# A Mamba-2 and pooling block on one core: the row's sums multiplied in front of the product for the state instead of behind it

## The chip, the core and the metric

The kernel runs on one core of a Trainium2 chip. The metric is the device time of one execution in microseconds (us). The time of a kernel is the median of several executions.

## What is computed

One layer of a decoder. Each of the 1024 prompt rows, and 8 samples of 8 rows, is normalised, projected by one large matrix, and sent through two branches: a causal pooling and a state-space recurrence (SSD). The branches are gated, added, projected once more and added to the input. The part that matters here is the recurrence. It goes over the prompt in chunks of 128 rows:

```python
def step(h, inp):
    xq, dq, Bq, Cq = inp
    acs = jnp.cumsum(dq * Ag, axis=1)
    seg = acs[:, :, None] - acs[:, None, :]
    decay = jnp.exp(jnp.where(mask, seg, -jnp.inf))
    cb = jnp.einsum('bign,bjgn->bijg', Cq, Bq)
    att = cb[..., None] * decay * dq[:, None]
    y = jnp.einsum('bijge,bjgep->bigep', att, xq)
    y = y + jnp.einsum('bign,bige,bgepn->bigep', Cq, jnp.exp(acs), h)
    last = acs[:, -1]
    w_in = jnp.exp(last[:, None] - acs) * dq
    h = h * jnp.exp(last)[..., None, None] + jnp.einsum('bjgn,bjge,bjgep->bgepn', Bq, w_in, xq)
    return h, y
```

`y` is the row's sums: one product within the chunk and one with the state `h` of the chunk before. The last line is the new state. The 32 heads are in 4 groups of 8 heads, each with its own B and C of 128 states.

## The kernel before

The kernel is one program of about 25,400 instructions in stages: the conditioned norm, the large projection, the samples' recurrence beside its end, then the **chunk rows** (about 765 to 1055 us of the span), and the last projections. The change lies in the chunk rows.

There are 32 chunks, 4 groups times 8 chunks, one after the other. `chunk(g, c)` (L1497) is a generator; each call of `next` puts one part of one chunk into the program:

- Part 0 loads the decays (L1234, by `decays`), B and C (L1502) and x (L1505), all on SP's queue.
- Part 1 takes the exponentials: `cE` on ScalarE (L1509), the mask on GpSimd (`far`, L1238), eight exponentials on ScalarE (`exps`, L1242). In the very first chunk these come later.
- Part 2 transposes x and B on TensorE (L1516, L1518), multiplies B with C (L1519), copies B to SBUF on ScalarE (`bt`, L1521) and C to PSUM (L1523), and lets VectorE make `xd` (L1527), `xw` (L1529), `dec` times B and C (L1534) and `cE` times C (L1536).
- Part 3 holds the change. The product for the state, `pu`, is one matmul of 512 columns into PSUM (L1541), recorded as two passes. The row's sums, `pi`, are made by `inner` (L1249): for each pair of heads two matmuls of 128 columns by 64 rows of `xd` (L1254) and, from the second chunk of a group on, two more with the state of the chunk before (L1257). VectorE then adds `pu` to the scaled old state (L1549; GpSimd scales it, L1547; in a group's first chunk ScalarE copies instead, L1545), and adds the skip term to `pi` in four instructions (L1553).
- Part 4 is `finish`: gating on VectorE (L1469), copies and squares on ScalarE (L1471, L1472), and sums on GpSimd (L1473 to L1480).

Between the parts stand **pieces** of other products (`products`, L1830; matmuls at L221): 12 matmuls each of 352 or 384 columns into one of three PSUM banks, emptied by VectorE or ScalarE (L1724, L1742, L1745). They fill TensorE while the other engines prepare the next chunk. In each step of the loop (L1849) TensorE gets the transposes of the next chunk, then about one piece, then `pu` and `inner` of this chunk, then one or two pieces.

What sets the order: TensorE's and SP's instructions are bound to the order in which the program is written (`in_line(order)`, L1910, with `ORDER`, L1837). The order on VectorE, ScalarE and GpSimd is made by the planner, which runs the program against computed times (`schedule_with_timeline_sim`, L19) and takes what is ready, earlier program text first.

Buffers: `pu` has one PSUM bank (`psC`), the transposes and `pi` share four (`psB`), the pieces have three (`psA`). `xw` has one SBUF buffer, so `xw` of the next chunk waits until this chunk's `pu` has been multiplied. `cE`, `xd` and the state have two, `dec` three.

Of the kernel before, what the change touches and what calls it, by code (L numbers as in the profile page):

```python
# [20 lines left out]
P = 128  # L21
# [25 lines left out]
def tile_pool_ssd_step(  # L47
# [8 lines left out]
    def nm(s):  # L56
        uid[0] += 1
        return f"{s}_{uid[0]}"
# [34 lines left out]
    def Y4(pool, dt=F32R):  # L93
        return pool.tile([P, 4, T], dt, tag="Y", name=nm("Y"), bufs=2)

    def PB():
        return psB.tile([P, 512], F32, tag="ps", name=nm("ps"))
# [4 lines left out]
    def PC():  # L102

        return psC.tile([P, 512], F32, tag="pc", name=nm("pc"))
# [1127 lines left out]
    def decays(dec, g, c):  # L1232

        load(dec, acs_d[c, 8 * g:8 * g + 8, :].partition_broadcast(P))  # L1234

    def far(dec, c):

        nc.gpsimd.affine_select(dec, dec, [[0, 8], [1, P]], ALU.is_ge, FAR, base=0, channel_multiplier=-1)  # L1238

    def exps(dec, g, c):  # L1240
        for h in range(8):
            act(dec[:, h], dec[:, h], AF.Exp, bias=acT[:, c, 8 * g + h:8 * g + h + 1], scale=-1.0)  # L1242
# [6 lines left out]
    def inner(xd, dec, S, state=None, cE=None):  # L1249
        pi = PB()  # L1250
        for q in range(4):
            o = [pi[64 * hh:64 * hh + 64, q * S:(q + 1) * S] for hh in range(2)]
            for hh in range(2):
                mm(o[hh], xd[:S, 2 * q + hh, :], dec[:S, 2 * q + hh], start=True, stop=state is None)  # L1254
            for hh in range(2 if state is not None else 0):
                h = 2 * q + hh
                mm(o[hh], state[:, h * 64:h * 64 + 64], cE[:, h], start=False, stop=True)  # L1257
        return pi[:, :4 * S].rearrange("p (q i) -> p q i", i=S)
# [201 lines left out]
    hst = [None] * NG  # L1460
# [3 lines left out]
    def ckt(shape, tag, bufs=2):  # L1464
        return (cl if tag in CKL else ca if tag in ("dec", "xb", "cE", "bc") else ck).tile(list(shape), F32, tag=tag, name=nm(tag), bufs=bufs)

    def finish(g, o, S, v, sz, y=None):

        V.tensor_tensor(v, v if y is None else y, sz, ALU.mult)  # L1469
        yhc = yh[g][:, :, o:o + S]  # L1470
        act(yhc, v, AF.Copy)  # L1471
        act(sz, v, AF.Square)  # L1472
        nc.gpsimd.tensor_tensor(yl[g][:, :, o:o + S], v, yhc.bitcast(F32), ALU.subtract)  # L1473
        nc.gpsimd.tensor_tensor(sz[:, 0:2], sz[:, 0:2], sz[:, 2:4], ALU.add)
        sa = sq_acc[:, o:o + S]
        if g == 0:
            nc.gpsimd.tensor_tensor(sa, sz[:, 0], sz[:, 1], ALU.add)
        else:
            nc.gpsimd.tensor_tensor(sz[:, 0], sz[:, 0], sz[:, 1], ALU.add)
            nc.gpsimd.tensor_tensor(sa, sa, sz[:, 0], ALU.add)  # L1480
# [16 lines left out]
    def chunk(g, c):  # L1497
        o = c * P
        dec = ckt([P, 8, P], "dec", 3)
        decays(dec, g, c)  # L1500
        bc = ckt([P, 2, P], "bc", 3)
        load(bc, xbc_d[g][c][:, 4:6])  # L1502
        Bf, Cf = bc[:, 0], bc[:, 1]
        xb = ckt([P, 4, P], "xb", 5)
        load(xb, xbc_d[g][c][:, 0:4])  # L1505
        yield
        if c > 0:
            cE = ckt([P, 8, P], "cE")
            act(cE, dec, AF.Exp, scale=-1.0)  # L1509
        if g > 0 or c > 0:  # L1510
            far(dec, c)
            exps(dec, g, c)
            yield
        px = PB()
        for q in range(4):
            nc.tensor.transpose(px[:, q * P:(q + 1) * P], xb[:, q], ident)  # L1516
        pbc = PB()
        nc.tensor.transpose(pbc[:, :P], Bf, ident)  # L1518
        mm(pbc[:, P:2 * P], Bf, Cf, start=True, stop=True)  # L1519
        bt = ckt([P, P], "bt", 2)  # L1520
        act(bt, pbc[:, :P], AF.Copy)  # L1521
        if c > 0:
            act(pbc[:, 2 * P:3 * P], Cf, AF.Copy)  # L1523
        pxv = px.rearrange("p (h d) -> p h d", d=64)
        heads = slice(8 * g, 8 * g + 8)
        xd = ckt([P, 8, 64], "xd", 2)
        V.tensor_tensor(xd, pxv, dtT[:, c, heads].unsqueeze(2).to_broadcast([P, 8, 64]), ALU.mult)  # L1527
        xw = ckt([P, 8, 64], "xw", 1)
        V.tensor_tensor(xw, pxv, wdT[:, c, heads].unsqueeze(2).to_broadcast([P, 8, 64]), ALU.mult)  # L1529
        if g == c == 0:  # L1530
            yield
            far(dec, c)
            exps(dec, g, c)
        V.tensor_tensor(dec, dec, pbc[:, P:2 * P].unsqueeze(1).to_broadcast([P, 8, P]), ALU.mult)  # L1534
        if c > 0:
            V.tensor_tensor(cE, cE, pbc[:, 2 * P:3 * P].unsqueeze(1).to_broadcast([P, 8, P]), ALU.mult)  # L1536
        yield
        if c == 0:
            yh[g], yl[g] = [Y4(hs if g % 2 else hp) for _ in range(2)]
        pu = PC()  # L1540
        mm(pu, bt, xw.rearrange("p h d -> p (h d)"), start=True, stop=True)  # L1541
        pi = inner(xd, dec, P, *((hst[g], cE) if c > 0 else ()))
        hn = ckt([P, 512], "hst", 2)
        if c == 0:
            act(hn, pu, AF.Copy)  # L1545
        else:
            nc.gpsimd.tensor_tensor(hn.rearrange("p (h d) -> p h d", d=64), hst[g].rearrange("p (h d) -> p h d", d=64),  # L1547
                                    Elb[:, c, heads].unsqueeze(2).to_broadcast([P, 8, 64]), ALU.mult)
            V.tensor_tensor(hn, hn, pu, ALU.add)  # L1549
        hst[g] = hn  # L1550

        for q in range(4):
            V.scalar_tensor_tensor(pi[:, q], xb[:, q], Dv[:, 4 * g + q:4 * g + q + 1], pi[:, q], ALU.mult, ALU.add)  # L1553
        yield
        finish(g, o, P, xb, szs.pop(0), pi)
        if c == NC - 1:
            store_(new_ssm_p[g], hn)
# [125 lines left out]
    def to_chunks():  # L1683
        nonlocal right, ca
        right.__exit__(None, None, None)
        right = tc.tile_pool(name="ca", bufs=3, side="right", reuse_waits="tile")
        ca = right.__enter__()
        right_all.append(right)
        seq.extend(chunk(g, c) for g in range(NG) for c in range(NC))
        next(seq[0])  # L1690
# [427 lines left out]
    for half in range(2):  # L2118
        c = slice(half * 512, half * 512 + 512)
# [168 lines left out]
```

## Time and profile before

| | |
|---|---|
| median of 3 runs | 1221.38 us (1220.97 to 1222.25) |
| the profiled execution | 1221.1 us |
| its span, first to last instruction | 1219.4 us |
| mean granted TensorE clock | 0.999 |
| DMA | 257.47 MB, mean 211 GB/s |

The profile is one execution of the program taken by the hardware profiler. PE is TensorE's matmuls, PEld its weight loads (they overlap PE), DVE is VectorE, ACT is ScalarE, POOL is GpSimd and SP is SyncE, which issues loads. A row of the timeline gives the start in us, the time in us, engine, line, operation, what it writes and reads, shapes, how many instructions are merged in it, and in brackets the idle time of its engine just before with what ended it. Rows of TensorE are merged where equal ones follow each other, and matmuls are pipelined: their ends overlap, so that the distance from start to start is what one costs.

### The profile page before, as it was taken

What the parts mean: (1) busy time and instruction counts of PE and PEld (TensorE: products, weight loads), DVE (VectorE), ACT (ScalarE), POOL (GpSimd) and SP (SyncE); (2) the same over time, 40 slices, a digit from 0 to 9 for tenths busy, and PEclk for the clock granted to TensorE, in tenths of its full rate; (3) what the DMA queues carried; (4) which work ended last, traced back from release to release, by engine and by line L of the source; (5) the groups of instructions that cost most, each with busy time, mean ns of one, the idle gap of its engine ahead of it and who ended that gap; (6) DMA issues with size and microseconds to landing.
All of it is one profiled execution on the core that took longest, in us unless ns stands there. A gap on an engine that the chain in (4) does not pass through costs nothing.

```text
span 1219.4 us, 25387 instructions
## 1 busy us (share of the span) xinstructions
PE 1204.5 (99%) x9298; PEld 1125.7 (92%) x9298; DVE 934.2 (77%) x1555; ACT 655.4 (54%) x1491; POOL 758.7 (62%) x677
## 2 busy tenths in 40 slices
PE   9999999999999999999999999999999999999997
PEld 8879999999999999999989889988988888999885
DVE  6993788877989578876676564686878889679976
ACT  6864366565656556454544344556676656312435
POOL 1137868876978778663676766155677758422661
PEclk9999999999999999999999999999999999999999
DMA  9736355564565546443555556897889888585794
GB/s 352 302 136 212 134 159 180 159 226 151 170 182 187 169 145 191 135 144 127 200 200 193 181 189 209 303 327 260 260 261 287 289 275 285 184 311 177 233 210 152
DMA packets 165748, 257.47 MB, mean 211 GB/s; under 512 B 32048, under 2 KB 79928, under 8 KB 165624
## 3 DMA queue, kind: packets, MB, share of 16 engines
q1 hardware_dynamic: 89256, 163.38, 40.9%
q10 hardware_dynamic: 74064, 88.27, 21.2%
q0 software_dynamic: 2304, 4.20, 2.0%
q8 instruction: 73, 1.20, 0.4%
q14 instruction: 51, 0.42, 0.1%
HBM read 170.69 MB, written 85.10 MB: 210 GB/s over the span
## 4 chain that ended last, share of the span: by engine, by line
PE 85%; DVE 5%; DMA 4%; ACT 3%; issue 2%; POOL 1%; SPq 0%; ACTq 0%; DVEq 0%; POOLq 0%
PE mm L410 23%; PE ps L410 23%; PE mm L221 15%; PE pc L410 5%; PE ps L1254 2%; PE pc L1541 2%; PE ps L2041 2%; PE ps L2040 2%; PE ps L1257 2%; PE ps L2039 2%; DMA dec<-acs_d 1%; DMA Y<-in_w_ada 1%; PE ps L1516 1%; PE ps L956 1%; DVE tf L642 1%
## 5 line engine op out<-in xcount | busy, mean ns | idle before, releaser
L148 POOL TENSOR_TENSOR wlo<-rawA,whi 128x512 fp32r<-128x512 f32 x120 | 173.3, 1450 | 80.2 <-ACT whi L145 78.9
L221 PE MATMUL mm<-Y,whi 128*128 128x352 f32 (+1 forms) x960 | 195.7, 334 | 0.8 <-DVE G L1974 0.6
L148 POOL TENSOR_TENSOR wlo<-raw,whi 128x512 fp32r<-128x512 f32 x90 | 149.8, 1673 | 61.3 <-ACT whi L145 54.0
L221 PEld LDWEIGHTS mm<-Y,whi 128*128 128x128 f32 x960 | 159.1, 188 | 7.6 <-issue 4.5
L1088 DVE SCALAR_TENSOR_TENSOR GA<-GA,cvT,GA 128x1112 f32<-128x1112 f32 x72 | 134.4, 1871 | 0.1
L410 PE MATMUL mm<-Y,whi 128*128 128x272 f32 x800 | 119.0, 291 | 0.0
L410 PE MATMUL ps<-Y,whi 128*128 128x272 f32 x800 | 117.4, 289 | 0.0
L145 ACT ACTIVATE whi<-rawA 128x512 fp32r<-128x512 f32 x120 | 75.2, 627 | 76.6 <-PE ps L410 32.4
L145 ACT ACTIVATE whi<-raw 128x512 fp32r<-128x512 f32 x90 | 56.0, 628 | 100.5 <-DVE raw L347 27.4
L410 PEld LDWEIGHTS mm<-Y,whi 128*128 128x128 f32 x800 | 106.8, 188 | 2.8 <-issue 2.4
L410 PEld LDWEIGHTS ps<-Y,whi 128*128 128x128 f32 x800 | 107.0, 188 | 0.8 <-issue 0.7
L221 PE MATMUL mm<-Y,wlo 128*128 128x352 f32 (+1 forms) x480 | 98.5, 327 | 0.0
L1242 ACT ACTIVATE dec<-dec,acT 128x128 f32<-128x128 f32 x256 | 78.7, 389 | 33.9 <-POOL dec L1238 33.9
L221 PEld LDWEIGHTS mm<-Y,wlo 128*128 128x128 f32 x480 | 81.7, 188 | 0.0
L285 POOL TENSOR_TENSOR pw<-pw,ph 128x512 fp32r<-128x512 f32 x40 | 67.1, 1678 | 13.2 <-ACT ph L283 12.7
L1473 POOL TENSOR_TENSOR Y<-xb,Y 128x512 fp32r<-128x512 f32 x32 | 41.2, 1289 | 53.8 <-ACT Y L1471 53.8
L410 PE MATMUL mm<-G,whi 128*128 128x272 f32 x480 | 71.4, 290 | 0.0
L410 PE MATMUL ps<-G,whi 128*128 128x272 f32 x480 | 70.5, 289 | 0.0
L410 PE MATMUL ps<-Y,wlo 128*128 128x272 f32 x400 | 66.6, 288 | 0.0
L410 PE MATMUL mm<-Y,wlo 128*128 128x272 f32 x400 | 66.6, 288 | 0.0
L410 PEld LDWEIGHTS mm<-G,whi 128*128 128x128 f32 x480 | 64.0, 188 | 1.3 <-issue 1.1
L410 PEld LDWEIGHTS ps<-G,whi 128*128 128x128 f32 x480 | 64.2, 188 | 0.4 <-issue 0.3
(579 smaller groups left out, 3155.3 us busy)
## 6 DMA issues: line engine op xcount, KB each, us to landing
rawA<-in_w_in SPq DMA_DIRECT2D x62, 512.0 KB
dec<-acs_d SPq DMA_DIRECT2D x32, 512.0 KB
xbc<-GA ACTq DMA_DIRECT2D x24, 512.0 KB
Y<-wo SPq DMA_DIRECT2D x10, 1024.0 KB
pw<-in_w_ssm_out ACTq DMA_DIRECT2D x32, 256.0 KB
ws<-ph ACTq DMA_DIRECT2D x32, 256.0 KB
ws<-pw ACTq DMA_DIRECT2D x32, 256.0 KB
h<-in_state_ssm SPq DMA_DIRECT2D x32, 256.0 KB
```

The lines of the kernel that those rows point to most:

```text
L145: ins = act(hi[:, :, :ncols], raw[:, :, :ncols], AF.Copy)
L148: (eng or nc.gpsimd).tensor_tensor(lo[:, :, :ncols], raw[:, :, :ncols], hi[:, :, :ncols].bitcast(F32), ALU.subtract)
L221: mm(ps[:, :n], w[k // 4][h][:, k % 4, :], r[k][:, o:o + n], start=(j == 0), stop=(j == len(terms) - 1))
L285: nc.gpsimd.tensor_tensor(raw.bitcast(F32R), raw, hi.bitcast(F32), ALU.subtract)
L410: mm(p, w[j // 8][:, k], A(k, s)[j // 4 == 1], start=(j == 0), stop=(j == 11))
L1088: V.scalar_tensor_tensor(d[:, :n], rp[:, k:k + n], cvT[:, 24 * k + mc:24 * k + mc + 1], d[:, :n], ALU.mult, ALU.add)
L1242: act(dec[:, h], dec[:, h], AF.Exp, bias=acT[:, c, 8 * g + h:8 * g + h + 1], scale=-1.0)
L1254: mm(o[hh], xd[:S, 2 * q + hh, :], dec[:S, 2 * q + hh], start=True, stop=state is None)
L1257: mm(o[hh], state[:, h * 64:h * 64 + 64], cE[:, h], start=False, stop=True)
L1473: nc.gpsimd.tensor_tensor(yl[g][:, :, o:o + S], v, yhc.bitcast(F32), ALU.subtract)
L1541: mm(pu, bt, xw.rearrange("p h d -> p (h d)"), start=True, stop=True)
L2039: mm(ps, hi, y[:, k, c0:c0 + cw], start=(first and k == 0), stop=False)
```

## The change

Two lines of part 3 change places. Before, TensorE multiplies `pu` and then the row's sums; afterwards the row's sums and then `pu`. Since TensorE's order is bound to the program's, its instructions change places with them. Nothing else is edited.

```diff
         pu = PC()
+        pi = inner(xd, dec, P, *((hst[g], cE) if c > 0 else ()))
         mm(pu, bt, xw.rearrange("p h d -> p (h d)"), start=True, stop=True)
-        pi = inner(xd, dec, P, *((hst[g], cE) if c > 0 else ()))
```

## The prediction

> **What bounds the kernel now.** I read the page first, then the stretch of the chunk rows, then the waits there, then single instructions in order of time.
>
> ```profile
> span 1219.4 us, 25387 instructions
> PE 1204.5 (99%) x9298; PEld 1125.7 (92%) x9298; DVE 934.2 (77%) x1555; ACT 655.4 (54%) x1491; POOL 758.7 (62%) x677
> 765.00:1055.00 290.00, 288.49 (x2296) 256.53 (x2295) 232.80 (x396) 179.75 (x467) 181.99 (x210) 1.00 0.84 279
> 1005.00:1035.00 30.00, 29.77 (x234) 26.09 (x232) 27.75 (x49) 20.41 (x54) 25.89 (x29) 1.00 0.86 285
> ```
>
> The last two rows are stretches: length, then busy time of PE, PEld, DVE, ACT and POOL, granted clock, DMA share. All 32 chunks lie in the first. PE is busy 288.49 of 290 us at clock 1.00, so it sets the pace, and at most 1.51 us of idle PE can be won here. DVE is busy 80% of the stretch and 27.75 of 30 us in its densest part: the engine that could become the bound.
>
> ```profile
> PE ps L1518 <- DVE cE L1536: 0.6, 1, 0.6
> PE mm L221 <- DVE Y L1572: 0.3, 1, 0.3
> PE ps L1254 <- DVE cE L1536: 0.2, 1, 0.2
> ```
>
> These are PE's longest waits in that stretch (us in total, times, longest); only two of the shortest size follow. The row's sums (L1254 and L1257, called the inner below) waited once, 0.2 us; the state's product (L1541, called pu) never. So before the change nothing stands still for pu's place in the queue.
>
> **Part 1: the same matmuls in another order.** The change removes and adds no instruction. Does the order itself cost PE time? One chunk, the thirteenth of 32 (chunk 12, counted from 0), with what surrounds it:
>
> ```profile
> 881.23 0.60 PE L1516 MATMUL ps<-ident,xb 128*128 128x128 f32 x4
> 881.66 0.27 PE L1518 MATMUL ps<-ident,bc 128*128 128x128 f32 x1
> 881.77 0.39 PE L1519 MATMUL ps<-bc 128*128 128x128 f32 x2
> ...
> 882.64 0.80 PE L221 MATMUL mm<-Y,wlo 128*128 128x352 f32 x4
> 883.28 0.80 PE L221 MATMUL mm<-Y,whi 128*128 128x352 f32 x4
> 883.92 1.02 PE L1541 MATMUL pc<-xw,bt 128*128 128x512 f32 x2
> 884.87 0.44 PE L1254 MATMUL ps<-dec,xd 128*64 128x128 f32 x4
> 885.14 0.39 PE L1257 MATMUL ps<-cE,hst 128*64 128x128 f32 x4
> 885.36 0.39 PE L1254 MATMUL ps<-dec,xd 128*64 128x128 f32 x4
> ...
> 886.45 0.39 PE L1257 MATMUL ps<-cE,hst 128*64 128x128 f32 x4
> 886.77 0.96 PE L221 MATMUL mm<-Y,whi 128*128 128x384 f32 x4
> 887.57 0.86 PE L221 MATMUL mm<-Y,wlo 128*128 128x384 f32 x4
> 888.26 0.34 PE L221 MATMUL mm<-Y,whi 128*128 128x384 f32 x1
> ```
>
> Matmuls overlap, so I take start to start. pu holds PE from 883.92 to 884.87, 0.95 us; the inner from 884.87 to 886.77, 1.90 us. What the changes of array shape (128*128 to 128*64 and back) cost:
> - Into the inner: four 128-column passes take 881.66 - 881.23 = 0.43, 0.11 each, so pu's two 512-column passes should take 2 x 0.43 = 0.86; they took 0.95, so +0.09. The inner's first four passes take 0.27, the next four 0.22: +0.05.
> - Out of it: the last four take 886.77 - 886.45 = 0.32, +0.10; the piece's first four 0.80 against 0.69 for the next four, +0.11.
>
> That is 0.35 us per chunk. Afterwards a piece stands in front of the inner and pu behind it. For the first, the trace has one place, a sample's inner behind a piece:
>
> ```profile
> 585.15 0.41 PE L410 MATMUL ps<-G,whi 128*128 128x272 f32 x2
> 585.40 0.67 PE L410 MATMUL ps<-G,wlo 128*128 128x272 f32 x4
> 585.99 0.68 PE L1254 MATMUL ps<-dec,xd 64*64 64x64 f32 x16
> ```
>
> Two matmuls take 0.25, so four should take 0.50; they took 0.59: again +0.09. The way out (0.10 + 0.11) now falls on pu. Behind pu a piece follows in the same shape, as behind L1519: from 881.77 to 882.64 are two passes and four piece matmuls, 0.22 + 0.64 = 0.86 expected, 0.87 taken. So there are two shape changes before and two after, and the order costs 0.01 x 32 = 0.3 us; I take 0. Not shown is what the first pass of pu does right behind the inner. If its long stream hides the 0.11 that the piece shows, 32 x 0.11 = 3.5 us are won; if piece and pu each show it, 3.5 us are lost. I take 0, since both rows that bear on it (the inner behind pu, and behind a piece) give the same surcharge.
>
> [...]
>
> **Part 2: the inner starts 0.95 us sooner.** It needs L1534 and L1536 (the decays times the products of B and C). Here are the closest places, on DVE and then on PE:
>
> ```profile
> 881.45 1.21 DVE L1536 TENSOR_TENSOR cE<-cE,ps 128x1024 f32<-128x1024 f32 x1
> 891.05 1.21 DVE L1536 TENSOR_TENSOR cE<-cE,ps 128x1024 f32<-128x1024 f32 x1
> 978.60 1.21 DVE L1536 TENSOR_TENSOR cE<-cE,ps 128x1024 f32<-128x1024 f32 x1
> 1014.05 1.21 DVE L1536 TENSOR_TENSOR cE<-cE,ps 128x1024 f32<-128x1024 f32 x1
> 1023.99 1.21 DVE L1536 TENSOR_TENSOR cE<-cE,ps 128x1024 f32<-128x1024 f32 x1
> ...
> 894.51 0.20 PEld L1254 LDWEIGHTS ps<-dec,xd 128*64 128x64 f32 x4 [0.76 <-issue]
> 981.56 0.44 PE L1254 MATMUL ps<-dec,xd 128*64 128x128 f32 x4
> 1017.32 0.44 PE L1254 MATMUL ps<-dec,xd 128*64 128x128 f32 x4
> 1024.10 1.02 PE L1541 MATMUL pc<-xw,bt 128*128 128x512 f32 x2
> 1025.35 0.44 PE L1254 MATMUL ps<-dec,xd 128*64 128x128 f32 x4 [0.23 <-DVE cE L1536]
> ```
>
> Start of the inner less end of L1536 (start + 1.21): 2.21 us for chunk 12, 2.25 for 13, 1.75 for 23, 2.06 for 27 and 0.15 for 28. Comparing every chunk in the same way, these five are the smallest. Less 0.95, four of them still have 0.80 to 1.30 us to spare. Chunk 28 has not: its inner already waits 0.23 us for L1536 while pu covers the time before. In front of the inner nothing covers it, so PE stands still some 0.95 us longer, and pu that follows gives nothing back. **Term: +0.95 us**, from 0 (if L1536 comes sooner there) to 0.95.
>
> Two things come sooner as well. The copy of the decays for a later chunk (L1509) waits until an inner has left its buffer, ten times in the trace; so does, by the code, the load of the decays, at the head of the chunk's loads in SP's queue (L1234, L1502, L1505, L1495):
>
> ```profile
> ACT cE L1509 <- PE ps L1257: 13.6, 10, 2.9
> ```
>
> Both move forward by up to 0.95 us, as does the inner that they serve, so the distance stays the same; I count 0. If it opened all that PE now waits for, it would bring the 1.5 us above. pu and the inner issue no DMA, so nothing else moves in the queues.
>
> **Part 3: pu ends 1.90 us later.** Then xw of the next chunk (L1529, one buffer) and the new state (L1549) come later.
>
> ```profile
> DVE xw L1529 <- PE pc L1541: 4.1, 7, 1.2
> 894.62 0.69 DVE L1529 TENSOR_TENSOR xw<-ps,wdT 128x512 f32<-128x512 f32 x1 [1.16 <-PE pc L1541]
> L1534 DVE TENSOR_TENSOR dec<-dec,ps 128x1024 f32<-128x1024 f32 x32 | 38.9, 1217 | 28.6 <-ACT ps L1523 13.6 <-POOL Y L1473 4.9 <-ACT dec L1242 4.1
> ```
>
> DVE stood still seven times for pu, up to 1.2 us, for xw. Behind xw in its queue are L1549, the four L1553, evictions of the pieces, L1534, L1536 and L1469; PE's next inner waits for L1534 and L1536. Each such wait may grow by 1.90. Against that stand the 28.6 us that DVE idles ahead of L1534 for other engines, where a delay disappears, and the planner: PE's and SP's orders are written out, but DVE's is planned anew from the times that the planner computes, and once the inner is first, the four L1553 are ready before xw and can fill the wait. The new state is read by the next inner, 9.6 us after this one (894.51 less 884.87), so its 1.90 matters only through the same queue. I take 0; the bound is the slower rival's sum below.
>
> **Sum:** 0 (order) + 0.95 (chunk 28) + 0 (sooner) + 0 (DVE). The profiled execution took 1221.1 us (span 1219.4 and 1.7 around it), 0.3 under the median of 1221.38. 1221.1 + 0.95 = 1222.05; as a median 1222.3 us. A difference under 0.2% (2.4 us) counts as no change here, so that is the forecast: **no change that a measurement tells**, its own range 1220 to 1223.7.
>
> **The rivals.**
>
> *Slower: DVE holds up the inner.* The place is xw's wait in DVE's queue, the price up to 1.90 us a chunk. If DVE keeps its order and the whole of it reaches L1536, the spare times turn negative: chunk 23 by 1.90 - 0.80 = 1.10, chunk 27 by 0.79, 12 by 0.64, 13 by 0.60, and chunk 28 by another 1.90. That is 5.0 us on top of 0.95: 1227.4 us. It decides from some 1.5 us of it on (2.4 less 0.95). For it speaks DVE's density (27.75 of 30 us) where two of the five lie; against it the 28.6 us of idle time ahead of L1534. [...]
>
> *Faster: PE itself runs better.* The 0.11 us of the piece behind the inner vanishes under pu's long passes: -3.5 us, with chunk 28 1221.38 - 3.5 + 0.95 = 1218.8 us; if the waits of 1.5 us go too, 1217.3. For it: pu's passes are four times as long as the inner's. Against it: the first pass still needs its own weights, and no row shows them hidden.
>
> *Nothing at all:* a new plan brings L1536 of chunk 28 sooner, no wait opens, 1221.4 us. Since PE's order is bound, the move itself does take place.
>
> **How the numbers follow.** Forecast 0.36, nothing at all 0.10, slower 0.33, faster 0.21. With the first two together: faster 0.21, within 0.2% 0.46, slower 0.33. The range from 1217.5 to 1229 takes in the faster case's sum nearly to its end, the slower one's 1227.4 and some waits of pieces behind a late DVE; about 2 in 10 lie outside.
>
> **What would show it.** Around 884 us the piece is followed by the inner after a step of about 0.25 (0.16 + 0.09), the inner lasts 1.90, pu follows, and the way from the inner's start to the fifth matmul of the next piece should be 3.56 us (887.57 - 884.87 + pu's 0.86). If it is 0.1 shorter in each chunk, the faster rival is right. PE's waits in the stretch should grow from 1.5 to about 2.5 us, with chunk 28's near 1.2 us on L1536. DVE's waits for pu ahead of xw should not grow much beyond 4.1 us, and L1553 should stand in front of xw at places; if they reach 10 us and more and PE's waits for L1534 or L1536 with them, the slower rival is right. The forecast is wrong if PE's idle time in the stretch is over 4 us or the stretch is shorter by 2.5.

## The result, and the profile after

The changed kernel takes 1227.63 us (median of 5 executions, 1226.34 to 1229.51); the kernel before, beside it, 1221.63 us (5 executions, 1220.97 to 1222.25). The ratio is 1.0049, 95% interval 1.0038 to 1.0059: slower by some 6 us. The forecast, no change that can be told, did not happen. The time is near that of the slower rival (1227.4), but, as the trace shows, the loss lies at another place than the rival named.

These are the page of the changed kernel and the two stretches that the prediction shows of before, with the same columns.

```profile
span 1227.8 us, 25373 instructions
PE 1207.2 (98%) x9298; PEld 1129.7 (92%) x9298; DVE 935.5 (76%) x1555; ACT 656.0 (53%) x1491; POOL 760.5 (62%) x677
765.00:1055.00 290.00, 283.92 (x2237) 253.98 (x2237) 228.64 (x387) 178.94 (x464) 179.25 (x206) 0.99 0.83 275
1005.00:1035.00 30.00, 30.00 (x258) 26.65 (x256) 27.72 (x48) 18.52 (x47) 23.65 (x27) 1.00 0.74 253
```

PE now idles 6.08 us of 290, before 1.51. The densest stretch of DVE, where the rival expected the harm, is clean: PE is busy for all of 30 us, and no wait of PE follows behind 1003 us, though the same work comes some 7 us later by then. The waits of PE between 765 and 1065 us (us in total, times, longest):

```profile
PE ps L1518 <- DVE ps L1553: 4.9, 3, 3.3
PE ps L1518 <- DVE cE L1536: 0.5, 1, 0.5
PE ps L1518 <- DVE dec L1534: 0.4, 1, 0.4
```

The 0.3 us at L221 is as before. All that grew waits at L1518, the transpose of B, and none at the inner. So PE has the operands of its sums in time; what it lacks is somewhere to put the next chunk's B. The largest of these waits, on PE's timeline:

```profile
876.98 0.86 PE L221 MATMUL mm<-Y,whi 128*128 128x384 f32 x4
877.76 0.44 PE L1254 MATMUL ps<-dec,xd 128*64 128x128 f32 x4
...
879.34 0.39 PE L1257 MATMUL ps<-cE,hst 128*64 128x128 f32 x4
879.66 1.12 PE L1542 MATMUL pc<-xw,bt 128*128 128x512 f32 x2
880.22 1.21 PE L221 MATMUL mm<-Y,whi 128*128 128x352 f32 x4
881.27 0.80 PE L221 MATMUL mm<-Y,wlo 128*128 128x352 f32 x4
...
882.55 0.60 PE L1516 MATMUL ps<-ident,xb 128*128 128x128 f32 x4
886.43 0.45 PE L1518 MATMUL ps<-ident,bc 128*128 128x128 f32 x1 [3.29 <-DVE ps L1553]
...
886.96 1.52 PE L221 MATMUL mm<-Y,whi 128*128 128x352 f32 x4
888.28 1.38 PE L221 MATMUL mm<-Y,wlo 128*128 128x352 f32 x4
...
898.17 0.60 PE L1516 MATMUL ps<-ident,xb 128*128 128x128 f32 x4
```

The transposes of x for chunk 13 start at 882.55; B should follow 0.43 us later and comes after 3.29 us of standstill. Then the piece's first four matmuls take 886.96 to 888.28, 1.3 us, where before they took 0.64. The granted clock says why (stretches of 2 us, the clock is the third number from the end; in the stretches ahead and behind these four it is 1.00):

```profile
884.00:886.00 2.00, 0.00 (x0) 0.00 (x0) 2.00 (x2) 1.05 (x2) 2.00 (x3) 0.77 0.69 236
886.00:888.00 2.00, 1.56 (x7) 1.60 (x8) 2.00 (x6) 1.66 (x6) 1.41 (x4) 0.50 0.00 0
888.00:890.00 2.00, 2.00 (x8) 2.00 (x8) 1.45 (x3) 0.96 (x4) 0.82 (x1) 0.50 0.00 0
890.00:892.00 2.00, 2.00 (x15) 1.62 (x16) 0.41 (x1) 1.14 (x4) 0.00 (x0) 0.52 0.00 0
```

TensorE stood still for 3.29 us and then ran at half clock until about 891.9, some 5.5 us; half of that, 2.7 us, is lost. The kernel before passes from the transposes of chunk 13 to those of chunk 14, and from those of the first chunk to those of the last, in these rows:

```profile
767.18 0.60 PE L1516 MATMUL ps<-ident,xb 128*128 128x128 f32 x4
...
890.88 0.60 PE L1516 MATMUL ps<-ident,xb 128*128 128x128 f32 x4
...
1038.92 0.60 PE L1516 MATMUL ps<-ident,xb 128*128 128x128 f32 x4
```

From chunk 13 to 14 it took 890.88 - 881.23 = 9.65 us before and 898.17 - 882.55 = 15.62 us after: 5.97 us more, 3.29 of them waiting and 2.68 at the lower clock. From the first chunk to the last the kernel before needs 271.74 us; the changed kernel's rows are:

```profile
767.82 0.60 PE L1516 MATMUL ps<-ident,xb 128*128 128x128 f32 x4
...
1046.89 0.60 PE L1516 MATMUL ps<-ident,xb 128*128 128x128 f32 x4
```

279.07 us, 7.33 more. PE's waits at L1518 sum to 5.8 us, before its waits in the chunks were 1.2 (the 0.6 and 0.2 that the prediction shows and two more of 0.2); 5.8 - 1.2 + 2.68 = 7.3. **So waits at L1518 and the clock behind the longest one are the whole loss of the chunk rows.** (The profiled execution is the slowest of the five, 1229.51 us, so that its loss is over the median's 6.0; it stands 8.4 us over the profiled execution before, and 1.1 of these lie outside the chunk rows, within the scatter of its executions.)

Why has L1518 no place to write? By the code the four PSUM banks of `psB` hold the transposed x of a chunk until `xd` and `xw` have read it, its transposed B until L1536, and its row's sums until L1469. At 882.98 one bank has just gone to chunk 13's x, and the other three still belong to chunk 12's x, chunk 12's B and chunk 11's sums. VectorE's rows in this place:

```profile
878.10 0.69 DVE L1527 TENSOR_TENSOR xd<-ps,dtT 128x512 f32<-128x512 f32 x1
...
883.83 1.22 DVE L1534 TENSOR_TENSOR dec<-dec,ps 128x1024 f32<-128x1024 f32 x1 [3.69 <-ACT ps L1523]
884.97 1.21 DVE L1536 TENSOR_TENSOR cE<-cE,ps 128x1024 f32<-128x1024 f32 x1
...
886.36 0.68 DVE L1529 TENSOR_TENSOR xw<-ps,wdT 128x512 f32<-128x512 f32 x1
```

`xd` of chunk 12 was made at 878.10. `xw` of chunk 12 could not follow at once, since the one xw buffer was in use by chunk 11's `pu`, which the change has moved to 879.66 (modelled end 880.78). It stands behind L1534 and L1536 in the queue, and L1534 waited for ScalarE until 883.83. DVE did nothing for 3.69 us, while `xw` had all it needed from 880.78 on. L1518 went on as soon as L1536 had let its bank go (884.97 + 1.21 = 886.18); the profile names L1553, which ran at that moment. In the kernel before, `xw` stood in front:

```profile
876.42 0.68 DVE L1527 TENSOR_TENSOR xd<-ps,dtT 128x512 f32<-128x512 f32 x1
...
878.39 0.68 DVE L1529 TENSOR_TENSOR xw<-ps,wdT 128x512 f32<-128x512 f32 x1
...
880.32 1.22 DVE L1534 TENSOR_TENSOR dec<-dec,ps 128x1024 f32<-128x1024 f32 x1 [0.65 <-ACT ps L1523]
```

Two things are different, then: `xw` is later and behind L1534, and ScalarE (L1523) is later. ScalarE's eight exponentials (L1242), which stand ahead of L1523 in its queue, start at 878.68 us, before at 874.00; they now come behind a copy of the split of w_o (L1776), for which ScalarE waited 2.02 us, by the profile for the store of an earlier copy. The second longest wait, 1.44 us at 1003.04, has the same form with another engine: `xw` (1002.96) stands behind an L1534 that waited 2.68 us for GpSimd. The experiments take the two apart.

### The profile page after: what moved, and what is told of

The parts are those of the page before. It is cut to its first block, busy times and chain, and to the rows that moved or that the text cites. A ratio compares the mean times of both kernels' runs of the same rounds, so it can differ in the third digit from the quotient of the medians.

```text
span 1227.8 us, 25373 instructions
## 1 busy us (share of the span) xinstructions
PE 1207.2 (98%) x9298; PEld 1129.7 (92%) x9298; DVE 935.5 (76%) x1555; ACT 656.0 (53%) x1491; POOL 760.5 (62%) x677
## 4 chain that ended last, share of the span: by engine, by line
PE 83%; DMA 5%; DVE 5%; ACT 4%; issue 1%; SPq 1%; POOL 1%; ACTq 0%; DVEq 0%
PE mm L410 23%; PE ps L410 23%; PE mm L221 14%; PE pc L410 5%; PE ps L1254 2%; PE pc L1542 2%; DMA dec<-acs_d 2%; PE ps L1257 2%; PE ps L2041 2%; PE ps L2040 2%; PE ps L2039 2%; ACT dec L1242 1%; DMA Y<-in_w_ada 1%; DMA R<-in_w_o 1%; PE ps L956 1%
## 5 line engine op out<-in xcount | busy, mean ns | idle before, releaser
L221 PE MATMUL mm<-Y,whi 128*128 128x352 f32 (+1 forms) x960 | 206.5, 345 | 0.8 <-DVE G L1974 0.6
L221 PEld LDWEIGHTS mm<-Y,whi 128*128 128x128 f32 x960 | 162.8, 189 | 17.4 <-issue 13.4
L410 PEld LDWEIGHTS mm<-Y,whi 128*128 128x128 f32 x800 | 106.8, 188 | 2.8 <-issue 2.4
L221 PE MATMUL mm<-Y,wlo 128*128 128x352 f32 (+1 forms) x480 | 99.0, 328 | 0.0
L1242 ACT ACTIVATE dec<-dec,acT 128x128 f32<-128x128 f32 x256 | 78.6, 389 | 25.6 <-POOL dec L1238 24.9
L221 PEld LDWEIGHTS mm<-Y,wlo 128*128 128x128 f32 x480 | 82.2, 189 | 0.0
L1473 POOL TENSOR_TENSOR Y<-xb,Y 128x512 fp32r<-128x512 f32 x32 | 41.8, 1306 | 43.0 <-ACT Y L1471 42.9
```

What stands on the lines that cost most here:

```text
L221: mm(ps[:, :n], w[k // 4][h][:, k % 4, :], r[k][:, o:o + n], start=(j == 0), stop=(j == len(terms) - 1))
L410: mm(p, w[j // 8][:, k], A(k, s)[j // 4 == 1], start=(j == 0), stop=(j == 11))
```

## The experiments

The letters in the expectations: A, the harm is one place, where the planner now puts the split of w_o (L1798, L1799) in front of the state's vector work around chunks 10 to 12; B, it is general, `pu` is late in every chunk and carries its lateness on through `xw`; C, it goes through the PSUM bank that `xw` holds. From e8 on, B is the one xw buffer, with the bank among its effects, and D is the rival that the state's chain and DVE's density cost the same with any buffers. Ratios and their intervals come from all executions of a run and of the kernel before beside it; they differ from the quotient of the two medians by up to 0.0007.

### e1, e2: the swap in some chunks only

```diff
+        first_ = g * NC + c == 10
+        if first_:
+            pi = inner(xd, dec, P, *((hst[g], cE) if c > 0 else ()))
         mm(pu, bt, xw.rearrange("p h d -> p (h d)"), start=True, stop=True)
+        if not first_:
+            pi = inner(xd, dec, P, *((hst[g], cE) if c > 0 else ()))
```

e1 swaps chunk 10 alone:

> Only chunk 10 has the new order, the other 31 the old. Theory A (one place: with pu of chunk 10 late, the planner puts the sums of the w_o split, L1798, which wait for a load, ahead of xw in VectorE's queue, everything behind it comes late, TensorE waits some 3.3 us for the bank of chunk 13's transposed B, and the idle time halves its clock for some 6 us): nearly the whole loss, 1226 to 1228 us. Theory B (pu's later end delays VectorE a little in every chunk): one thirty-second of the loss, 1221.6 to 1222.2 us.

e2 swaps all but chunks 9 to 12 (`first_ = not 9 <= g * NC + c <= 12`):

> Chunks 9 to 12 have the old order, the other 28 the new. Theory A: the sums of the w_o split stand behind the state again in the plan, the long wait and the half clock vanish, 1222 to 1224.5 us. Theory B: 28 of 32 parts of the loss remain, 1226 to 1227.5 us.

e1: 1223.75 us beside 1222.31 of before, ratio 1.0019 (1.0009 to 1.0029). e2: 1221.4 us, 0.9992 (0.9982 to 1.0001). PE's longest wait in the chunk rows, e1:

```profile
PE ps L1518 <- DVE ps L1557: 1.7, 1, 1.7
```

and e2:

```profile
PE ps L1518 <- DMA dec<-acs_d: 1.3, 1, 1.3
```

(e1's profile is of the fastest of its ten executions, 1221.5 us, so that it may show less than the median lost.) 28 of the 32 swaps together cost nothing; one alone costs 1.4 us, again at L1518, two chunks after the swap. So a swap has no price of its own; it matters where it tips the plan over. e1 fell short of A's 1226 and above B's 1222.2, and e2 came out under both ranges, so neither theory had its size.

### e3, e4: the split of w_o held back

```diff
-            V.tensor_tensor(dn[:, right_], dn[:, right_], up[:, right_], ALU.subtract)
-            V.tensor_tensor(up[:, right_], up[:, right_], up[:, left_], ALU.subtract)
+            with behind(mybir.EngineType.DVE, 5):
+                V.tensor_tensor(dn[:, right_], dn[:, right_], up[:, right_], ALU.subtract)
+                V.tensor_tensor(up[:, right_], up[:, right_], up[:, left_], ALU.subtract)
```

The two lines are L1798 and L1799. `behind` binds an instruction behind an earlier one of the engine, here the sixth last that the program has written for DVE. e3 does this in the changed kernel, e4 in the kernel before.

> The new order in all chunks, but the two sums at the head of each w_o step (L1798, L1799) may be planned only behind the state's sum L1549 of the chunk before them. Theory A: no wait over 2 us, no half clock, 1222 to 1225 us. Theory B: nothing changes, 1226.5 to 1229 us.

> Control: the same restriction on the w_o step in the kernel before. Both theories: within 1 us of the kernel before, 1221 to 1222.6 us.

e3: 1228.21 us, ratio 1.0048 (1.0033 to 1.0063), no better than the change. e4: 1220.86 us, 0.9987 (0.9978 to 0.9997), a little under the expected 1221. e3's longest waits of PE, and the clock behind the one of them that ended at 980.89:

```profile
PE ps L1518 <- DVE cE L1536: 5.6, 2, 3.5
```

```profile
982.00:984.00 2.00, 2.00 (x8) 2.00 (x7) 2.00 (x5) 1.30 (x5) 1.68 (x2) 0.51 1.04 365
984.00:986.00 2.00, 2.00 (x21) 1.56 (x21) 1.97 (x5) 1.15 (x4) 0.00 (x0) 0.64 0.31 117
```

The wait at chunk 13 is gone, and two others of the same kind have come, 2.07 us in front of chunk 24's B and 3.52 in front of chunk 29's. In both, `xw` again stands behind an L1534 that waits, 2.46 and 3.93 us for ScalarE. So A falls as the whole cause: the place isn't chunk 13, it is L1518 wherever the plan is tight.

### e5, e6: xw without the PSUM bank

```diff
-        V.tensor_tensor(xw, pxv, wdT[:, c, heads].unsqueeze(2).to_broadcast([P, 8, 64]), ALU.mult)
+        V.tensor_tensor(xw, xd, wdT[:, c, heads].unsqueeze(2).to_broadcast([P, 8, 64]), ALU.mult)
...
-            V.tensor_tensor(wd[:n, f], wd[:n, f], dt[:n, f], ALU.mult)
+            if n == NS:
+                V.tensor_tensor(wd[:n, f], wd[:n, f], dt[:n, f], ALU.mult)
```

`xd` is x times dt already, so `xw` is made from it in SBUF and the bank is free after `xd`. e5 is the changed kernel, e6 the one before.

> The new order; xw is made from xd in SBUF (times the exponential alone) and no longer from the transposes' PSUM bank. xw still waits for pu's end. Theory C (the place is the bank for the next chunk's transposed B: L1518 gets it when the first of xw, L1536 and L1469 lets one of three banks go; with pu last, xw lets go up to 1.9 us later, so TensorE waits at L1518, over 3 us where the w_o split loads the queues): xd frees the bank early, TensorE's waits at L1518 fall from 5.8 to under 1 us, no stretch at half clock, 1220.5 to 1222.5 us. Theory B (VectorE's and ScalarE's queues are late as such): waits of 3 us and more remain somewhere, 1226 to 1229 us.

> The same change of xw in the kernel before, old order. Theory C: its 0.8 us of waits at L1518 vanish, 1220 to 1221.6 us. Theory B: no difference, 1221 to 1222.5 us.

e5: 1225.71 us beside 1221.33, ratio 1.0033 (1.0022 to 1.0044). e6: 1222.98 us, 1.001 (1.0001 to 1.0018). Neither theory has its time: e5 lies between the two ranges, and e6 above both. The new order costs 2.7 us in this pair instead of 6.0. e5's longest waits of PE, and its `xw` among DVE's groups of that stretch (the mean in ns behind the comma):

```profile
PE ps L1258 <- DVE hst L1550: 2.4, 4, 1.2
PE ps L1255 <- DVE cE L1537: 2.2, 2, 1.3
```

```profile
L1530 DVE TENSOR_TENSOR xw<-xd,wdT 128x512 f32<-128x512 f32 x32 | 29.9, 933 | 0.0
```

No wait at L1518 is left: the bank part of C is right. But `xw` takes 933 ns instead of 683, which fills DVE by 32 x 0.25 = 8 us, and there are now waits for the state and for cE. e6, in the old order, has them too: 2.1 us at `pu` for the state and 1.5 us at the inner for cE. So a good part of them comes with the dearer `xw`; what the new order adds to them this pair leaves open.

### e7: no idle time at chunk 13

```diff
+        for _ in range(14 if g * NC + c == 13 else 0):
+            mm(px[:, :P], ident, ident, start=True, stop=True)
         for q in range(4):
             nc.tensor.transpose(px[:, q * P:(q + 1) * P], xb[:, q], ident)
```

Fourteen matmuls more in the changed kernel, whose results the transposes overwrite.

> The new order; in front of chunk 13's transposes 14 more matmuls of 128 columns (3.05 us at 0.109 us a pass, their result is overwritten) stand where TensorE waited 3.3 us. If idle time halves the clock: no half clock behind them, the place costs 3.3 us and not 6, 1224.5 to 1226 us when nothing else moves. If the half clock has another cause: it stays, 1227 to 1229.5 us.

1226.82 us, ratio 1.0041 (1.0026 to 1.0056), between the two ranges. The stretches in which the changed kernel had 0.77 and 0.50:

```profile
884.00:886.00 2.00, 1.57 (x15) 1.33 (x13) 2.00 (x2) 1.09 (x2) 2.00 (x3) 1.00 0.45 163
886.00:888.00 2.00, 1.53 (x11) 1.56 (x12) 1.97 (x6) 1.61 (x6) 1.43 (x4) 1.00 0.00 0
```

With the standstill broken up the clock stays at 1.00, so it was the idle time that halved it. The time doesn't tell what that is worth, since the added work moved the plan and other waits came, 3.2 us beside the 0.3 at L221.

### e8, e9, e10: a second xw buffer

```diff
-        sz = ckt([P, 4, NS], "szs", 1)
+        sz = scT.rearrange("p k s -> p (k s)").rearrange("p (q s) -> p q s", s=NS)
-        v = ckt([P, 4, NS], "v", 1)
+        v = ElS.rearrange("p b h -> p (b h)").rearrange("p (q s) -> p q s", s=NS)
...
-        xw = ckt([P, 8, 64], "xw", 1)
+        xw = ckt([P, 8, 64], "xw", 2)
```

The first two edits put two tiles of the samples' end into tiles that nothing reads any more by then (`scT`, `ElS`) and so make room for the third. e8 is the changed kernel with all, e9 the kernel before with all, e10 the changed kernel with the room made and one xw buffer.

> The new order in all chunks, with two buffers for xw instead of one, so that xw (L1528) of a chunk no longer waits for pu of the chunk before; the room comes from two dead tiles that the samples' end now uses. Theory B (the one xw buffer carries pu's 1.90 us into DVE's queue and into the bank that L1518 waits for): about as before, 1220.5 to 1222.5 us, no wait of PE at L1518 over 1 us, DVE's waits for pu ahead of xw gone. Theory D (what is late is the state's chain, pu to hst to the next pu, and DVE's queue is too full whatever the buffers; the run with xw made from xd still lost 2.7 us against its partner): 1224 to 1227 us, with waits of PE for hst (L1549) and cE.

> The kernel before with the same second xw buffer. Both theories: 1219.5 to 1222 us, within 0.1% of before; DVE's waits for pu ahead of xw (4.1 us in the stretch before) go, and PE had 1.5 us of waits to lose. If it is slower than before by over 2 us, the plan behind the buffer does more than the wait itself, and the run with the new order has to be read against this one.

> The new order with the samples' end put into the two dead tiles, and still one xw buffer: the control for the second buffer. Theories B and D: as the changed kernel, 1226 to 1229 us, with a wait of PE at L1518 or at other places behind cE and xw of 2 us and more. If it is at 1221 to 1223 us, the moves and not the second buffer made the difference.

Beside 1221.86 us of before: e8 1222.9 us, ratio 1.0002 (0.9993 to 1.001); e9 1220.74, 0.9991 (0.9982 to 1.0); e10 1227.69, 1.0051 (1.0038 to 1.0064). e8 lies just above B's range and below D's. The control loses all that the change lost; with a second buffer 4.8 us of it are gone. Here is e8's PE in the place where the changed kernel stood still:

```profile
881.85 0.27 PE L1518 MATMUL ps<-ident,bc 128*128 128x128 f32 x1
...
885.82 0.44 PE L1254 MATMUL ps<-dec,xd 128*64 128x128 f32 x4 [1.55 <-DVE cE L1536]
886.58 0.44 PE L1257 MATMUL ps<-cE,hst 128*64 128x128 f32 x4 [0.32 <-DVE hst L1549]
```

The transpose of B passes, the piece is done, and PE waits only at the inner, for L1536. DVE in the same place:

```profile
877.35 0.68 DVE L1529 TENSOR_TENSOR xw<-ps,wdT 128x512 f32<-128x512 f32 x1
...
883.32 1.22 DVE L1534 TENSOR_TENSOR dec<-dec,ps 128x1024 f32<-128x1024 f32 x1 [4.32 <-ACT ps L1523]
```

`xw` is in front again, 9 us sooner than in the changed kernel, although L1534 waits for ScalarE longer still, 4.32 us. So the buffer, not ScalarE, sets when the bank is free; ScalarE's lateness is the second cause: its exponentials stand here too behind a copy of the split of w_o (L1776 at 877.13 us), for which it waited 3.27 us. That it costs what is left is tested next.

### e11, e12: both

e11 is the kernel before, e12 the changed one, each with the second xw buffer and with the split of w_o held back as in e3.

> The kernel before with two xw buffers and with the split of w_o (L1798, L1799) put where DVE is free behind the state's vector work. Each alone measured 0.9991 and 0.9987 of before, at the edge of what can be told. If the waits they remove are different ones, together 1218.5 to 1220.8 us (0.998); if DVE's queue in these chunks only trades one wait for another, 1220.5 to 1222, no better than either alone.

> The new order with both. Theory B (with two buffers the place of pu costs nothing): as its partner with the old order, within 0.1%, 1219 to 1222 us. If the new order still costs something of its own (the run with two buffers stood 2 us over its partner, most of it one wait of 1.55 us for cE in chunk 13, behind the split of w_o): more than 1.5 us over its partner, 1221.5 to 1224 us, with such a wait at another chunk.

Beside 1221.31 us of before: e11 1219.49 us, ratio 0.9988 (0.9979 to 0.9996); e12 1219.7 us, 0.9985 (0.9976 to 0.9994). The two can't be told apart, and both are a little faster than the kernel before. The only wait of PE over 0.15 us that is left in the chunk rows is the 0.3 of a first piece (L221) that every version has. First and last transposes of x, e11:

```profile
767.35 0.60 PE L1516 MATMUL ps<-ident,xb 128*128 128x128 f32 x4
...
1037.14 0.60 PE L1516 MATMUL ps<-ident,xb 128*128 128x128 f32 x4
```

and e12:

```profile
767.05 0.60 PE L1516 MATMUL ps<-ident,xb 128*128 128x128 f32 x4
...
1036.69 0.60 PE L1516 MATMUL ps<-ident,xb 128*128 128x128 f32 x4
```

269.79 and 269.64 us. Where nothing waits, 32 swaps change the time by 0.15 us.

All corners, as medians in us (each beside its own runs of before, which lay between 1221.3 and 1222.3):

| | old order | new order | new less old |
|---|---|---|---|
| one xw buffer, w_o as planned | 1221.63 | 1227.63 | 6.0 |
| one xw buffer, w_o held back (e4, e3) | 1220.86 | 1228.21 | 7.4 |
| two xw buffers, w_o as planned (e9, e8) | 1220.74 | 1222.9 | 2.2 |
| two xw buffers, w_o held back (e11, e12) | 1219.49 | 1219.7 | 0.2 |

By the ratios the third row's difference is 0.0011, 1.3 us, and the last one's -0.0003. Holding w_o back alone does nothing for the new order; the second buffer takes most of the loss, and both take all. D falls with the last row.

## Why the prediction was right, and where it was wrong

The forecast, 1222.3 us and 1220 to 1223.7 as its own range, missed by 5.3 us, and its sign of being wrong came: PE's idle time in the stretch is 6.08 us, over 4. The wider range, 1217.5 to 1229, holds the time only because it takes in the slower rival.

**Part 1, the order on PE, 0 us: right.** From the inner's start to the fifth matmul of the piece behind `pu` the changed kernel takes 881.27 - 877.76 = 3.51 us. The prediction's 3.56 was worked out with a piece of 384 columns; four of 352 take 0.05 less (0.64 for 0.69). The inner follows the piece after 0.78 for four passes of 0.69, the 0.09 of before; `pu` follows the inner after 0.32 for 0.22, its 0.10. The 0.11 that a piece showed behind the inner is still there, behind `pu`: `pu` and four passes of the piece take 881.27 - 879.66 = 1.61 us for 0.86 + 0.64. So nothing is hidden, e11 and e12 differ by 0.15 us over 32 chunks, and the faster rival falls.

**Part 2, chunk 28 waits 0.95 us more: did not happen.** Its rows are now, on DVE

```profile
1030.51 1.21 DVE L1536 TENSOR_TENSOR cE<-cE,ps 128x1024 f32<-128x1024 f32 x1
```

and on PE

```profile
1032.46 0.44 PE L1254 MATMUL ps<-dec,xd 128*64 128x128 f32 x4
```

L1536 ends at 1031.72 and the inner starts 0.74 us later without waiting. PE had by then lost over 7 us elsewhere, which gave the other engines time to catch up; that this is the reason is not shown. The wait depends on the plan: in e7, also in the new order, this inner did wait for the same product (L1538 there), 0.78 us, and in e12, where nothing is lost ahead of it, it didn't wait. A spare time read in the old trace holds only as long as nothing in front of it moves.

**Part 3, `pu` 1.90 us later, taken as 0: this is the step that failed.** The prediction followed `xw` forward, from the wait for `pu` through DVE's queue to L1534 and L1536. It did not follow what `xw` holds while it waits: the bank of the transposed x, which L1518 of the next chunk needs. The buffers are named ahead of the prediction, four banks for the transposes and the sums, and PE's longest wait of before, 0.6 us, already stood at L1518. The planner did move `xw` out of the way, as Part 3 hoped, so that DVE hardly waits for `pu` at all. The groups of DVE in the stretch, after and before:

```profile
L1529 DVE TENSOR_TENSOR xw<-ps,wdT 128x512 f32<-128x512 f32 x32 | 21.9, 683 | 0.5 <-PE pc L1542 0.5
```

```profile
L1529 DVE TENSOR_TENSOR xw<-ps,wdT 128x512 f32<-128x512 f32 x32 | 21.9, 683 | 4.2 <-PE pc L1541 4.1
```

DVE's idle time ahead of `xw` fell from 4.2 to 0.5 us: the sign that was to show the slower rival went the other way, and the kernel still became slower. Moving `xw` back behind L1534 saved DVE's time and kept the bank, 5.6 us at chunk 12 (880.78 to 886.36).

**The slower rival**: its cause in outline, `pu`'s later end reaching PE through `xw`, was right; its place (the inner, at five chunks) and its way (`xw` in front, holding up L1536) were not. So it is luck that its sum, 1227.4, meets the time: none of its waits at the inner occurred, and the loss is made of waits at L1518 and a lower clock. DVE's queue did hold up what PE needed, though with the parts changed: it was `xw` that stood behind an L1534 that waited 3.69 us, with all it needed for the last 3.05 of them (880.78 to 883.83). By these rows an instruction that lets a buffer go is better not placed behind one that waits for another engine.

**Not in any sum: the clock.** 2.68 of the 5.97 us at chunk 13 came after the wait, at half clock. The prediction priced a wait at its own length.

What stays open: that the new plan puts L1798 in front because `pu` leaves DVE free there is only argued from the order of the rows; what the half clock alone is worth was not separated in time (e7).

## What to carry to other kernels

When an instruction is moved back, list the buffers that it and those who wait for it still hold, PSUM banks above all, and look who takes the next one; a bank that comes free late stops TensorE, whose order is bound to the program's here, at a harmless transpose (for 3.29 us at chunk 13), far from the operands that one watches. A single buffer between a producer that a planner places and a consumer that is moved is the first thing to double. And where TensorE sets the pace, a wait may cost much of its length again in clock (2.68 us behind 3.29 here) or nothing more (1.44 us, near 1003 us).

## What the hardware showed

In these runs the length of an idle time alone did not tell whether the clock fell. Single waits of 1.44 us (the changed kernel, near 1003 us) and 1.68 us (e1, near 875 us) left it at 1.00; 2.07 us (e3, chunk 24) were followed by stretches of 0.51 and 0.64, 3.29 us in the changed kernel by 0.50. Two waits of 0.94 and 1.21 us, 0.44 us apart, left it at 1.00 in e5 (near 886 us). In e8 two waits, 1.55 and 0.32 us, also 0.44 us apart, were followed by these:

```profile
886.00:888.00 2.00, 1.68 (x22) 1.43 (x21) 2.00 (x5) 2.00 (x8) 1.71 (x3) 0.76 0.00 0
888.00:890.00 2.00, 2.00 (x15) 1.53 (x12) 1.86 (x3) 1.98 (x7) 0.28 (x1) 0.50 0.02 2
```

With start and end estimated from the mean clock of the first and last stretch (of 2 us, of 4 us in e3's second place), the half clock lasts about 3.4 us in e8 (887.05 to 890.5) and in both places of e3 (982.0 to 985.4, 1029.8 to 1033.2), and about 6.8 us, twice that, in the changed kernel (885.1 to 891.9) and in e10 (884.9 to 891.7). By the start TensorE had stood still for 1.9 us (e8, both waits), 2.0 (the changed kernel), 2.1 and 3.4 (e3) and 2.6 (e10), though the start came up to 1.1 us after the wait's end. What sets the start and the two lengths is not shown: no run shifts a wait to test it.

The same product of 512 elements a row took VectorE 683 ns with x from PSUM and 933 ns on average (e5; 861 in e6) with `xd` from SBUF. The traces of e5 and e6 show the difference instruction by instruction: of the 64 products 37 took 0.68 or 0.69 us, as from PSUM. The other 27, up to 1.72 us, all began while a GpSimd instruction was running, and 26 of them ended 0.53 to 0.55 us behind its end (for the last one, two GpSimd rows are merged). Of the 37 one began 0.01 us after a GpSimd instruction that then ran for 1.63 us; the others found none running, or one with at most 0.13 us to go. The changed kernel has the same at L1805, whose two operands are in SBUF too: at 921.13 it took 1.78 us and ended 0.54 us behind a GpSimd instruction (L1473, 920.55 to 922.37); at 967.64, with none running, it took 0.68. So in these runs the product from SBUF wasn't slower by itself; those that took longer were the ones beside GpSimd's work.
